# A streaming SwiGLU kernel: rows packed four to a slot, 64 KiB store descriptors, all transfers on one queue

## The chip, the cores and the metric

One core of a Trainium2 chip. Times are device microseconds (us) of whole executions; the profile's span is about 1.8 us shorter than the time of the same execution.

## The reference

```python
x = np.random.randn(8192, 8192).astype(np.float32)   # fixed seed
a, b = np.split(x, 2, axis=-1)
out = a * (b / (1 + np.exp(-b)))                      # 8192 x 4096 float32
```

268.4 MB are read, 134.2 MB are written, and each element is computed once.

## The kernel before

Two rows of x lie side by side in each of the 128 partitions (64 KiB), three such slots take turns. ACT computes silu in place, DVE multiplies in place, and the result is stored from the slot's front half. Loads are issued from the SP queue, nearly all stores from the ACT queue.

```python
R, BUFS = 2, 3
xv = x.tensor.reshape([N // R, R * M]).ap()
ov = out.tensor.reshape([N // R, R * half]).ap()
...
def load(i, rows=None):          # SP queue, 128 x 64 KiB
    ...
    nc.sync.dma_start(out=tiles[i][:, lo*M : hi*M], in_=xv[i*P : (i+1)*P, lo*M : hi*M])

def store(i, c0=0, cw=R * half): # ACT queue, 128 x 32 KiB
    (nc.scalar if i < last - 1 else nc.sync).dma_start(
        out=ov[i*P : (i+1)*P, c0 : c0+cw], in_=tiles[i][:, c0 : c0+cw])

for i in range(BUFS):
    load(i)
for i in range(last):
    for k in range(R):
        swiglu(i, k)             # ACT silu in place, DVE multiply in place
    ...
    store(i)
    nxt = i + BUFS
    if nxt < last:
        load(nxt)                # waits until store(i) has landed
    ...                          # the last tile is loaded and stored in pieces
```

Of the kernel before, what the change touches and what calls it, by code (L numbers as in the profile page):

```python
# [1 line left out]

# [4 lines left out]

_SILU = mybir.ActivationFunctionType.Silu


@with_exitstack
def kernel(
    ctx: ExitStack,
    tc: tile.TileContext,
    x: bass.AP,
    out: bass.AP,
):




    nc = tc.nc
    N, M = x.shape
    half = M // 2
    P = nc.NUM_PARTITIONS
    R = 2
    BUFS = 3

    xv = x.tensor.reshape([N // R, R * M]).ap()  # L30
    ov = out.tensor.reshape([N // R, R * half]).ap()
    ntiles = N // (P * R)
    last = ntiles - 1

    pool = ctx.enter_context(tc.tile_pool(name="sbuf", bufs=BUFS))
    ctx.enter_context(tc.manual_schedule())
    tiles = {}

    def load(i, rows=None):
        if i not in tiles:  # L40
            tiles[i] = pool.tile([P, R * M], x.dtype, name="xt")
        lo, hi = (0, R) if rows is None else rows
        nc.sync.dma_start(  # L43
            out=tiles[i][:, lo * M : hi * M], in_=xv[i * P : (i + 1) * P, lo * M : hi * M]
        )

    def swiglu(i, k, c0=0, cw=half):
        xt = tiles[i]
        b = xt[:, k * M + half + c0 : k * M + half + c0 + cw]
        nc.scalar.activation(out=b, in_=b, func=_SILU)  # L50
        nc.vector.tensor_mul(  # L51
            out=xt[:, k * half + c0 : k * half + c0 + cw],
            in0=xt[:, k * M + c0 : k * M + c0 + cw],
            in1=b,
        )

    def store(i, c0=0, cw=R * half):
        (nc.scalar if i < last - 1 else nc.sync).dma_start(
            out=ov[i * P : (i + 1) * P, c0 : c0 + cw], in_=tiles[i][:, c0 : c0 + cw]
        )  # L60

    for i in range(BUFS):
        load(i)
    for i in range(last):
        for k in range(R):
            swiglu(i, k)
        if i == last - 1:
            swiglu(last, 0)
        store(i)
        nxt = i + BUFS  # L70
        if nxt < last:
            load(nxt)
        elif nxt == last:
            load(last, (0, 1))
            load(last, (1, 2))

    store(last, 0, half)
    for c0 in range(0, half, half // 2):
        swiglu(last, 1, c0, half // 2)
    store(last, half, half)  # L80


# [1 line left out]
_INS = ['x']  # L84
_OUTS = [((8192, 4096), 'float32')]


# [23 lines left out]
```

## Time and profile before

| | before |
|---|---|
| time, median | 936.1 us |
| span of the profiled run | 934.8 us |
| busy: DVE, ACT | 30%, 25% |
| DMA engines, in 100 to 880 us | share 1.00, 434 to 435 GB/s |
| bytes moved | 402.67 MB |
| store on ACT queue, issue to landing | 39.7 us, one every 29 us |

Read it as a transfer-bound kernel: the 16 DMA engines never rest, and the computing fits beside them three times over. The lines behind the table stand in the prediction.

### The profile page before, as it was taken

Reading aid. Unit: us, or ns where it says so; the run is one execution under the profiler, and the core shown is the slowest. Engines: PE = TensorE matmul, PEld = TensorE weight load, DVE = VectorE, ACT = ScalarE, POOL = GpSimd, SP = SyncE. Lnnn points to the kernel's source line nnn. Section 1 sums busy time; section 2 is a strip of 40 time slices with the busy share of each in tenths; the row PEclk is TensorE's granted clock in tenths of the full one; section 3 lists DMA queues with packets and bytes.
Section 4 is the critical chain, followed back from the end, with each engine's and each line's share of the span. In section 5 each row is a group of like instructions: output and inputs, shape, how many; then the busy total and the mean of one; then the engine's idle time right before and its main releaser. Section 6 shows DMA issues by size and latency. Waiting matters only on the chain.

```text
span 934.8 us, 367 instructions
## 1 busy us (share of the span) xinstructions
DVE 283.3 (30%) x65; ACT 229.4 (25%) x66; POOL 0.2 (0%) x4
## 2 busy tenths in 40 slices
DVE  0333312333123331133321333213332133331242
ACT  0223320233302333113331133311333203332041
POOL 0000000000000000000000000000000000000000
DMA  9999999999999999999999999999999999999998
GB/s 404 400 445 430 430 439 433 428 435 443 428 430 439 429 442 432 435 426 453 419 430 452 411 452 423 428 447 425 433 433 453 414 443 429 426 447 428 425 437 376
DMA packets 9506, 402.67 MB, mean 431 GB/s; under 512 B 1056, under 2 KB 1056, under 8 KB 1056
## 3 DMA queue, kind: packets, MB, share of 16 engines
q1 hardware_dynamic: 5184, 276.83, 68.6%
q10 hardware_dynamic: 4320, 125.83, 31.2%
q14 instruction: 2, 0.02, 0.0%
HBM read 268.44 MB, written 134.22 MB: 431 GB/s over the span
## 4 chain that ended last, share of the span: by engine, by line
DMA 84%; DVE 10%; ACT 4%; DVEq 0%; issue 0%; SPq 0%; ACTq 0%
DMA out_dram<-xt 42%; DMA xt<-in_x_dram 42%; DVE xt L51 10%; ACT xt L50 4%; DVEq L106 0%; SPq L43 0%; ACTq L50 0%; DVEq L51 0%
## 5 line engine op out<-in xcount | busy, mean ns | idle before, releaser
L51 DVE TENSOR_TENSOR xt<-xt 128x4096 f32<-128x4096 f32 (+1 forms) x65 | 283.3, 4359 | 637.7 <-ACT xt L50 634.5
L50 ACT ACTIVATE xt<-xt 128x4096 f32<-128x4096 f32 (+1 forms) x65 | 228.1, 3556 | 688.1 <-DMA xt<-in_x_dram 688.1
L50 ACT ACT_TABLE_LOAD x1 | 1.3, 1283 | 0.7 <-PEq L95 0.7
L95 POOL MEMSET const-bfloat16-1.0<- 128x1 bf16 x1 | 0.1, 103 | 0.0
L95 POOL MEMSET const-uint8-127<- 128x1 uint8 x1 | 0.1, 102 | 0.0
L95 POOL MEMSET const-float32-0.0<- 128x1 f32 x1 | 0.1, 100 | 0.2 <-issue 0.2
L95 POOL MEMSET const-float32-1.0<- 128x1 f32 x1 | 0.1, 99 | 0.0
## 6 DMA issues: line engine op xcount, KB each, us to landing
out_dram<-xt ACTq DMA_DIRECT2D x30, 4096.0 KB, 39.7
xt<-in_x_dram SPq DMA_DIRECT2D x2, 4096.0 KB, 27.1
out_dram<-xt SPq DMA_DIRECT2D x1, 4096.0 KB, 23.6
out_dram<-xt SPq DMA_DIRECT2D x2, 2048.0 KB, 14.5
xt<-in_x_dram SPq DMA_DIRECT2D x31, 34.5
```

The lines of the kernel that those rows point to most:

```text
L50: nc.scalar.activation(out=b, in_=b, func=_SILU)
L51: nc.vector.tensor_mul(out=xt[:, k * half + c0 : k * half + c0 + cw], in0=xt[:, k * M + c0 : k * M + c0 + cw], in1=b,)
L95: nc = _bacc.Bacc("TRN2", target_bir_lowering=False, num_devices=1)
```

## The change

Intent: a store of four rows at once has 64 KiB per partition instead of 32 KiB, so there are half as many store descriptors. For this, four rows are loaded in two loads (the "pack" and the "extra"), and the results of the extra are written by DVE into the half of the pack that has become free. All transfers go to the SP queue in the order store, extra load, pack load.

```diff
-    R = 2
-    BUFS = 3
+    ngroups = N // (4 * P) - 1
...
+    extra = pool.tile([P, 2 * M], x.dtype, name="extra")
+    packs = [pool.tile([P, 2 * M], x.dtype, name=f"pack{s}") for s in range(2)]
...
+    load_pack(0)
+    load_extra(0)
+    load_pack(1)
+    for g in range(ngroups):
+        pack = packs[g % 2]
+        for k in range(2):
+            swiglu(pack, k, pack, k)
+        for k in range(2):
+            swiglu(extra, k, pack, 2 + k)
+        rows = o4[g * P : (g + 1) * P, :]
+        nc.sync.dma_start(out=rows, in_=pack)
+        load_extra(g + 1)
+        if g + 2 <= ngroups:
+            load_pack(g + 2)
...  (the last two tiles are loaded and stored in pieces, as before)
```

More of the change, by code (lines that the diff above doesn't have):

```diff
@@ L26 @@
     P = nc.NUM_PARTITIONS
-    R = 2
-    BUFS = 3
-    xv = x.tensor.reshape([N // R, R * M]).ap()
-    ov = out.tensor.reshape([N // R, R * half]).ap()
-    ntiles = N // (P * R)
-    last = ntiles - 1
-    pool = ctx.enter_context(tc.tile_pool(name="sbuf", bufs=BUFS))
-    ctx.enter_context(tc.manual_schedule())
-    tiles = {}
-    def load(i, rows=None):
-        if i not in tiles:
-            tiles[i] = pool.tile([P, R * M], x.dtype, name="xt")
-        lo, hi = (0, R) if rows is None else rows
-        nc.sync.dma_start(
-            out=tiles[i][:, lo * M : hi * M], in_=xv[i * P : (i + 1) * P, lo * M : hi * M]
-        )
@@ L47, in swiglu @@
-    def swiglu(i, k, c0=0, cw=half):
-        xt = tiles[i]
-        b = xt[:, k * M + half + c0 : k * M + half + c0 + cw]
+    ngroups = N // (4 * P) - 1
+    x4 = x.tensor.reshape([N // 4, 4 * M]).ap()
+    o4 = out.tensor.reshape([N // 4, 4 * half]).ap()
+    x2 = x.tensor.reshape([N // 2, 2 * M]).ap()
+    o2 = out.tensor.reshape([N // 2, 2 * half]).ap()
+    pool = ctx.enter_context(tc.tile_pool(name="sbuf", bufs=1))
+    ctx.enter_context(tc.manual_schedule())
+    extra = pool.tile([P, 2 * M], x.dtype, name="extra")
@@ L50, in swiglu @@
+    packs = [pool.tile([P, 2 * M], x.dtype, name=f"pack{s}") for s in range(2)]
+    def swiglu(src, k, dst, d, c0=0, cw=half):
+        b = src[:, k * M + half + c0 : k * M + half + c0 + cw]
         nc.scalar.activation(out=b, in_=b, func=_SILU)
         nc.vector.tensor_mul(
-            out=xt[:, k * half + c0 : k * half + c0 + cw],
-            in0=xt[:, k * M + c0 : k * M + c0 + cw],
+            out=dst[:, d * half + c0 : d * half + c0 + cw],
+            in0=src[:, k * M + c0 : k * M + c0 + cw],
@@ L54, in swiglu @@
             in1=b,
         )
-    def store(i, c0=0, cw=R * half):
-        (nc.scalar if i < last - 1 else nc.sync).dma_start(
-            out=ov[i * P : (i + 1) * P, c0 : c0 + cw], in_=tiles[i][:, c0 : c0 + cw]
-        )
-    for i in range(BUFS):
-        load(i)
-    for i in range(last):
-        for k in range(R):
-            swiglu(i, k)
-        if i == last - 1:
-            swiglu(last, 0)
-        store(i)
-        nxt = i + BUFS
-        if nxt < last:
-            load(nxt)
-        elif nxt == last:
-            load(last, (0, 1))
-            load(last, (1, 2))
@@ L77, with load_pack, load_extra @@
-    store(last, 0, half)
+    def load_pack(g):
+        if g < ngroups:
+            src = x4[g * P : (g + 1) * P, : 2 * M]
+        else:
+            src = x2[2 * ngroups * P : (2 * ngroups + 1) * P, :]
+        nc.sync.dma_start(out=packs[g % 2], in_=src)
+    def load_extra(g):
+        if g < ngroups:
+            nc.sync.dma_start(out=extra, in_=x4[g * P : (g + 1) * P, 2 * M :])
+        else:
+            r0 = (2 * ngroups + 1) * P
+            for k in range(2):
+                nc.sync.dma_start(
+                    out=extra[:, k * M : (k + 1) * M], in_=x2[r0 : r0 + P, k * M : (k + 1) * M]
+                )
@@ new lines @@
+    load_pack(0)
[5 more added lines that the diff above has]
+            swiglu(pack, k, pack, k)
+        for k in range(2):
+            swiglu(extra, k, pack, 2 + k)
[4 more added lines that the diff above has]
+            load_pack(g + 2)
+    pack = packs[ngroups % 2]
+    r0 = 2 * ngroups * P
+    for k in range(2):
+        swiglu(pack, k, pack, k)
@@ L78 @@
+    swiglu(extra, 0, extra, 0)
+    nc.sync.dma_start(out=o2[r0 : r0 + P, :], in_=pack[:, :M])
+    r0 += P
+    nc.sync.dma_start(out=o2[r0 : r0 + P, :half], in_=extra[:, :half])
     for c0 in range(0, half, half // 2):
-        swiglu(last, 1, c0, half // 2)
-    store(last, half, half)
+        swiglu(extra, 1, extra, 1, c0, half // 2)
+    nc.sync.dma_start(out=o2[r0 : r0 + P, half:], in_=extra[:, half:M])
 _INS = ['x']
```

## The prediction

> **What bounds the kernel now.** I read the slices of the page first, then the table by stage, then the timeline of one stage, then the waits.
>
> The slices and the DMA part of the page:
>
> ```profile
> DVE  0333312333123331133321333213332133331242
> ACT  0223320233302333113331133311333203332041
> DMA  9999999999999999999999999999999999999998
> DMA packets 9506, 402.67 MB, mean 431 GB/s; under 512 B 1056, under 2 KB 1056, under 8 KB 1056
> q1 hardware_dynamic: 5184, 276.83, 68.6%
> q10 hardware_dynamic: 4320, 125.83, 31.2%
> ```
>
> See that the 16 DMA engines are busy in all 40 slices, while DVE and ACT are idle for about 70%. The two queues' packets fill 68.6 + 31.2 = 99.8% of the engines' time: no second resource hides behind them.
>
> The table by stage (stretch and its length, busy time of DVE, ACT, POOL, clock, DMA share, GB/s):
>
> ```profile
> 0.00:1.00 1.00, 0.00 (x0) 0.28 (x1) 0.20 (x4) 1.00 0.00 0
> 23.40:46.70 23.30, 8.85 (x2) 6.59 (x3) 0.00 (x0) 1.00 0.99 401
> 100.00:500.00 400.00, 123.91 (x28) 99.72 (x28) 0.00 (x0) 1.00 1.00 435
> 500.00:880.00 380.00, 115.05 (x26) 92.59 (x26) 0.00 (x0) 1.00 1.00 434
> 932.00:934.80 2.80, 0.00 (x0) 0.00 (x0) 0.00 (x0) 1.00 0.07 29
> ```
>
> See that 780 of the 935 us run at a DMA share of 1.00 and 434 to 435 GB/s. Only the edges differ: no transfer in the first microsecond (the second has them), 401 GB/s in the stretch in which the first store meets the loads, and almost nothing in the last 2.8 us.
>
> The timeline of one stage gives the beat of the loop:
>
> ```profile
> 220.52 7.12 ACT L50 ACTIVATE xt<-xt 128x4096 f32<-128x4096 f32 x2 [21.89 <-DMA xt<-in_x_dram]
> 224.16 8.96 DVE L51 TENSOR_TENSOR xt<-xt 128x4096 f32<-128x4096 f32 x2 [20.06 <-ACT xt L50]
> 233.15 0.34 ACTq L58 DMA_DIRECT2D out_dram<-xt  x1
> 249.51 7.12 ACT L50 ACTIVATE xt<-xt 128x4096 f32<-128x4096 f32 x2 [21.87 <-DMA xt<-in_x_dram]
> ```
>
> See a new tile every 249.51 - 220.52 = 28.99 us. From a tile's landing to the issue of its store are 233.15 - 220.52 = 12.63 us, and after that ACT waits 21.9 us for the next load.
>
> The waits, of the compute engines and of the SP queue:
>
> ```profile
> ACT xt L50 <- DMA xt<-in_x_dram: 688.1, 33, 22.5
> SPq L43 <- DMA out_dram<-xt: 869.3, 29, 67.8
> ```
>
> See that SP nearly always waits for a store to land before it may reload that slot. This looks like a slot shortage, but the DMA share of 1.00 says that other queued transfers cover it. The chain of waits (42% store, 42% load) is that same queueing seen through the slots.
>
> The whole is 32 tiles x 28.99 = 927.7 us, and 7.1 us of edges. Of these about 2.0 lie before the first byte, about 1.8 in the slow stretch (23.3 x (1 - 401/434)), about 2.6 at the end (2.8 x 0.93), and some 0.7 are unassigned.
>
> **What the Trainium skill says.** First, "DMA: Bandwidth & Descriptors", section "Where 436 GB/s comes from": 16 ports x 32 B x 850 MHz make 435.2 GB/s. The trace agrees (434 to 435 in the steady stages). Bytes moved are 402.65 MB, so an estimate of the floor from that figure is 402.65 MB / 435.2 GB/s = 925.2 us. The kernel is 9.6 us of span, 1%, above a floor that includes no start, no end and no descriptor cost.
>
> Second, the same page, "Issuing engines are not separate DMA queues": issuing from several engines saves only the sequencer's issue time, as all run on the same 16 DMA engines. The trace agrees: in the steady stages a load descriptor takes the same 2418 ns whether or not the other queue has work, and the engines alternate without a gap. One issue costs 0.33 us, off the path.
>
> Third, the same page, "Latency and other measured facts", row "HBM row pitch at large powers of two": copies of 16 KiB rows at a pitch of 512 KiB between partitions ran at 207 GB/s a direction, against a full 214, and far lower at 2 MiB and more. The change loads rows of 64 KiB at a pitch of 128 KiB, where before the pitch was 64 KiB. No run here shows that pitch yet; it is below the smallest that the row found slow.
>
> **The change part by part.**
>
> *Bytes.* None removed: x is read once and out is written once. This caps everything at the 1% above.
>
> *Store descriptors.* The one thing truly removed. The packet records have three sizes, with medians of 2418 ns for 64 KiB, 1213 ns for 32 KiB, 611 ns for 16 KiB. Two halves cost 2 x 1213 = 2426, so joining two saves 8 ns on one engine. Per group of four rows (two tiles of before), an engine does 16 loads x 2418 + 16 stores x 1213 = 58.10 us before, and 16 x 2418 + 8 x 2418 = 58.03 us after; with one completion packet of 9 ns fewer the saving is 0.073 us, and over 15 groups 1.1 us. A second working, from the beat: two tiles take 57.98 us, 0.16 us above 25.17 MB / 435.2 GB/s = 57.83; spread over 32 descriptors and 4 completions that is 4.4 ns each, 9 of them fewer per group, 0.04 us, 0.6 us over 15 groups. I take 0.9 us.
>
> *Compute.* The order of instructions shows the same 65 activations of mean 3556 ns and 65 multiplications of mean 4359 ns; the last two of each four multiplications read the extra tile and write the pack. Change in time: none.
>
> *Slots and waits.* Still 192 KiB a partition (two packs, one extra), but other waits. Call the transfers of group g S (store), E (extra load), P (pack load). SP issues S(g), E(g+1), P(g+2). S(g) and E(g+1) both wait until the extra of g is computed; P(g+2) waits until S(g) has landed. All three are 8.39 MB, 8 descriptors an engine, 8 x 2418 = 19.34 us. Does the one queue ever run dry?
> - When E(g) lands, P(g+1) is next in the queue and covers 19.34 us. The store is issued 12.63 us later, and its first byte follows about 1.25 us after issue (first load issued at 0.73, first bytes at about 2.0). That is 13.9 us; slack 19.3 - 13.9 = 5.4 us, less a microsecond for the landing to be seen and up to 2 for engines ahead of others. About 3 us are left.
> - When S(g) lands, E(g+1) covers 19.34 us, and P(g+2) needs 0.33 + 1.25. Slack about 17 us.
> So every wait is covered and adds 0.
>
> *Moved: the store issue from ACT to SP.* ACT loses 30 issues of 0.34 us, about 10 us, but it idles 688 us. Worth 0. SP blocks in order, but S(g+1) cannot be ready before P(g+2) has been issued: S(g) lands about one transfer before E(g+1).
>
> *Edges.* The start is the same three loads of 8.39 MB. At the end, when the last half load lands, there are 4.19 + 2.10 + 2.10 MB of stores to run, as now, 19.3 us, and the last computing (about 8 us) fits beside the first 14.5. Change 0.
>
> Sum: 936.1 - 0.9 = **935.2 us**.
>
> **The rivals.**
>
> *A: turns between loads and stores cost time.* Before, load and store descriptors alternate on two queues, and stores are never absent once begun: each takes 39.7 us to land, and a new one comes every 29. The only turn from loads alone to stores, in 23.4 to 46.7, costs 1.5 to 1.8 us. After, each engine turns twice per group: 8 loads' or stores' worth of one kind, then the other. If each of 15 turns to stores cost 1.6 us, the time would be 935.2 + 14 x 1.6 = 958 us, slower by 2.3%. Against it: before, each engine switches between the kinds at nearly every descriptor at 435 GB/s, so a switch as such is free, and in the tail load and store descriptors follow each other on one queue without a gap. A little, 0.1 us a turn, would make 938.
>
> *B: the queue runs dry behind S.* The 3 us of slack could be smaller than thought, if landing is seen late. Missing 1 us per group would make 935 + 15 = 950; but compute durations are steady to some 20 ns, and I see nothing that takes 3 us. If only the engines that are ahead run dry, the end doesn't move.
>
> *C: the pitch of 128 KiB slows loads.* At the 3% that the skill's row has at 512 KiB, two thirds of the time would grow: 620 x 0.03 = 19 us, 954 us. For it: only the similar power of two. Against it: the pitch is four times smaller.
>
> *D: a little is gained at the edge.* The first store now queues behind a load rather than breaking in beside it; if that removes the 1.6 us, 933.6.
>
> **Range and chances.** Main path 80%: 933.5 to 936. Small costs of A to C 14%: up to 940. One of them in full 5%: about 950 to 958. Faster than 917.4 would need less than the floor of 925.2, so 1%, for a misread. Range 933 to 938.5; faster 0.01, same 0.94, slower 0.05.
>
> **What would show it.** Right: DMA nines throughout; about 57.9 us from one group to the next (activation of extra to the next); one queue only, at 99.7% of the engines, with the store descriptors at 2418 ns. Issue to landing about 26 us for the store (some 5 left of P, 19.3, 1), 45 for the extra, 39 for the pack. SP waits for DVE before the store and for the store before the pack load. The chain of waits is led by the extra load, with two multiplications (15%) and an activation (6%) per group. Wrong: a DMA share under 0.98 in the steady stages (B), descriptors over 2418 ns at each turn (A), or loads over 2418 ns throughout (C).

## The result, and the profile after

| | before | after |
|---|---|---|
| time, median of 6 runs | 936.29 us | 940.9 us |
| lowest to highest | 935.9 to 937.33 | 940.35 to 942.11 |
| span of the profiled run | 934.8 us | 938.6 us |

The ratio is 1.0049, interval 1.0037 to 1.0062. Ratios in this document are the mean time of one kernel's fast runs over that of the other's in the same rounds, so not quite the ratio of the medians quoted. The change is half a percent slower: inside 2%, but outside the predicted range of 933 to 938.5, and on the other side of the kernel before.

The slices and queues of the page, then the DMA issues (count, KB where given, median us from issue to landing):

```profile
DMA  9999999999999999999999999999999999999997
q1 hardware_dynamic: 7344, 402.66, 99.5%
...
pack<-in_x_dram SPq DMA_DIRECT2D x16, 38.8
extra<-in_x_dram SPq DMA_DIRECT2D x15, 45.2
out_dram<-pack SPq DMA_DIRECT2D x15, 26.4
```

One queue now fills the engines, and the three latencies are those foreseen (39, 45, 26). The waits (total, times, longest, us) and the chain's shares by engine:

```profile
ACT extra L44 <- DMA extra<-in_x_dram: 483.7, 17, 32.1
...
SPq L80 <- DVE pack L45: 471.3, 15, 31.7
SPq L57 <- DMA out_dram<-pack: 360.7, 14, 27.1
```

```profile
DMA 77%; DVE 14%; ACT 6%; SPq 1%; issue 0%; DVEq 0%; ACTq 0%
```

SP waits for the last multiplication before a store and for the store before a pack load, as in the working. The schedule does what it was designed to do, and yet the span grew by 3.8 us.

The chain of waits in order of time, with the lines that begin each group's extra (start us, us, what):

```profile
101.47 3.62 ACT extra L44
...
160.22 3.63 ACT extra L44
...
218.97 3.62 ACT extra L44
...
277.85 3.63 ACT extra L44
...
394.68 3.62 ACT extra L44
...
452.65 3.62 ACT extra L44
...
510.83 3.63 ACT extra L44
...
568.83 3.62 ACT extra L44
```

The early groups take 160.22 - 101.47 = 58.75 us, then 58.75 and 58.88; from 394.68 on 57.97, 58.18 and 58.00. Two tiles of before took 57.98. So the loop loses 0.8 us a group in the beginning, then almost nothing. A cost that fades is not the cost of a size or of an address.

The table by stage has the second loss, at the end (the line of before stands in the prediction: 2.8 us at 0.07):

```profile
100.00:500.00 400.00, 123.28 (x28) 99.72 (x28) 0.00 (x0) 1.00 1.00 433
...
932.00:938.60 6.60, 0.00 (x0) 0.00 (x0) 0.00 (x0) 1.00 0.26 109
```

For its last 6.6 us the kernel moves 109 GB/s: a few of the 16 engines still have descriptors to move while the others have finished.

The trace's packet records tell which. They can be strung together into 16 chains, one for each engine, since a packet starts within a few ns of the end of the one before (459 packets each after, 594 before, 25.17 MB, idle by some 0.3 us at most). A string can swap two engines, so the values for the worst engine are rough. "Lengthening" below is the sum, over an engine's packets, of what they took beyond the usual 2418, 1213 or 611 ns:

```
                                              before   after
lengthening, mean of the 16 engines, us         2.18    4.60
lengthening, the worst engine, us               3.2     8
last engine's end minus the mean end, us        1.26    3.34
first to last engine's end, us                  1.81    4.71
```

The mean grew by 2.4 us and the lag of the last engine by 2.1; 4.5 us, less the 0.6 to 1.1 that fewer descriptors were reckoned to save, gives the 3.8 measured. After the first 0.77 us at the start of the kernel, the lengthening sits almost wholly in one place: the last load descriptor ahead of each store, where an engine turns from loading to storing.

```
turn (group)             1     2     3     4     5     6     7     8
mean lengthening, us   1.07  0.44  0.19  0.29  0.36  0.20  0.10  0.05
engines apart by, us    0.5   1.0   1.3   2.0   3.4   3.6   3.6   3.4
```

("Apart" is the spread of the engines' starts on that descriptor.) At first all 16 engines turn within half a microsecond and all pay. Then they drift apart, and mainly those that come late go on paying: summed over the 16 turns, the eight earliest pay 2.6 us each and the four latest 5.3 us. The kernel before has one such place, its first store: about 1.5 us there, and 0.05 us in all afterwards.

### The profile page after: what moved, and what is told of

Same layout as the page of the kernel before. It is cut to its first block, busy times and chain, and to the rows that moved or that the text cites. A ratio compares the mean times of both kernels' runs of the same rounds, so it can differ in the third digit from the quotient of the medians.

```text
span 938.6 us, 324 instructions
## 1 busy us (share of the span) xinstructions
DVE 281.9 (30%) x65; ACT 229.4 (24%) x66; POOL 0.2 (0%) x4
## 4 chain that ended last, share of the span: by engine, by line
DMA 77%; DVE 14%; ACT 6%; SPq 1%; issue 0%; DVEq 0%; ACTq 0%
DMA extra<-in_x_dram 77%; DVE pack L45 14%; ACT extra L44 6%; SPq L80 1%; DVE extra L45 0%; DVEq L121 0%; SPq L66 0%; SPq L57 0%; ACTq L44 0%; SPq L62 0%
## 5 line engine op out<-in xcount | busy, mean ns | idle before, releaser
L45 DVE TENSOR_TENSOR pack<-extra 128x4096 f32<-128x4096 f32 x30 | 131.4, 4422 | 427.7 <-ACT extra L44 427.7
L44 ACT ACTIVATE extra<-extra 128x4096 f32<-128x4096 f32 (+1 forms) x33 | 114.2, 3505 | 483.7 <-DMA extra<-in_x_dram 483.7
L45 DVE TENSOR_TENSOR pack<-pack 128x4096 f32<-128x4096 f32 x32 | 141.6, 4425 | 191.0 <-ACT pack L44 189.3
L44 ACT ACTIVATE pack<-pack 128x4096 f32<-128x4096 f32 x32 | 114.0, 3608 | 208.2 <-DMA pack<-in_x_dram 208.2
L45 DVE TENSOR_TENSOR extra<-extra 128x2048 f32<-128x2048 f32 (+1 forms) x3 | 8.9, 3001 | 24.1 <-ACT extra L44 24.1
## 6 DMA issues: line engine op xcount, KB each, us to landing
pack<-in_x_dram SPq DMA_DIRECT2D x16, 38.8
extra<-in_x_dram SPq DMA_DIRECT2D x15, 45.2
out_dram<-pack SPq DMA_DIRECT2D x15, 26.4
```

Source lines behind the costliest of these rows:

```text
L44: nc.scalar.activation(out=b, in_=b, func=_SILU)
L45: nc.vector.tensor_mul(out=dst[:, d * half + c0 : d * half + c0 + cw], in0=src[:, k * M + c0 : k * M + c0 + cw], in1=b,)
```

## The experiments

Two rival theories stood at the start. **T1**: what costs is a store phase that begins on all engines together after a stretch of loads, whatever the queue. **T2**: what costs is a load followed by a store on one ring. And **T3**: the packing itself, by pitch or by descriptor size. The first four runs shared a chip and the runs of before (936.12 us).

### Stores on the ACT queue

```diff
-        nc.sync.dma_start(out=rows, in_=pack)
+        nc.scalar.dma_start(out=rows, in_=pack)
```

> The changed kernel with the 15 group stores issued from the ACT queue, nothing else changed. The packet records of the changed kernel show no idle engine, but the last load descriptor ahead of each store phase lengthened (1.07 us at the first turn, 0.45, 0.19, 0.29, 0.36 at the next ones, fading later), most on one or two engines that end 4 us late. T1, store phases that begin on all engines together after a stretch without stores slow the loads in flight, whatever the queue: the stores still pause some 19 us in each 58 us group, so the time stays at 939 to 942 and the lengthened load descriptors stay. T2, a load followed by a store on one ring is what costs: two rings interleave as in the kernel before, the lengthening goes except at the very first store, 934.5 to 936. T3, the 64 KiB store descriptors or the 128 KiB pitch cost: as the changed kernel, 940.5 to 941.5, with the lengthening spread over all descriptors of that kind.

Measured: 968.22 us, ratio 1.0346. Neither theory expected this: the lengthening does not stay or go but grows, to 24.6 us on average over the engines. SP's waits and the timeline show what came on top:

```profile
SPq L57 <- DMA out_dram<-pack: 616.5, 14, 50.2
```

```profile
156.98 0.33 SPq L57 DMA_DIRECT2D pack<-in_x_dram  x1
159.42 7.12 ACT L44 ACTIVATE extra<-extra 128x4096 f32<-128x4096 f32 x2 [27.04 <-DMA extra<-in_x_dram]
```

The store shares the engines with the extra load and lands late, so the next pack load is issued only 2.4 us before the extra load has been seen to land. The engines stood idle for 9.8 us on average in the whole run. So the run doesn't decide against T2: some engines ran dry, and that is what the lengthening goes with. After the first store (1.2 us) there are 14 more turns. Between the load ahead of the turn being issued and the turn itself, no engine was idle in two of them, and the turn cost 0.10 and 0.04 us on average over the engines; in the other 12 at least two engines were, and it cost 0.89 to 1.66. Another 6 us or so lie at the restarts themselves. The engines began these stores 0.7 to 3.1 us apart, so the cost did not need all of them to turn at one moment.

### The same schedule without the packing

```diff
-            src = x4[g * P : (g + 1) * P, : 2 * M]
+            src = x2[2 * g * P : (2 * g + 1) * P, :]
...  (the extra likewise from tile 2g+1)
-        nc.sync.dma_start(out=rows, in_=pack)
+        for h in range(2):
+            nc.sync.dma_start(out=o2[(2*g+h)*P : (2*g+h+1)*P, :], in_=pack[:, h*M : (h+1)*M])
```

> The changed kernel's schedule and single queue, but with the row mapping of the kernel before: each load is 128 x 64 KiB from one contiguous 8.39 MB block, and the group store is two stores of 128 x 32 KiB. No packing, no 64 KiB store descriptor, no 128 KiB pitch is left. T1 and T2 (the phase order or the single ring costs): 940 to 942, lengthened load descriptors ahead of the store phases remain. T3 (pitch or descriptor size): back to 935.5 to 937.

Measured: 939.79 us, ratio 1.0040. No 64 KiB store and no 128 KiB pitch is left, and nearly all of the cost remains (1.0049 and, in a later batch, 1.0036 for the changed kernel). T3 falls: the mapping isn't what costs. In the records the first turn costs 1.2 us, and the later ones don't simply fade: the sixth costs 0.56 and the tenth 0.32. Whether 30 stores of 32 KiB descriptors are slower than 15 of 64 KiB can't be told from the time at this noise.

### The kernel before on one queue

```diff
-        (nc.scalar if i < last - 1 else nc.sync).dma_start(
+        nc.sync.dma_start(
...
         store(i)
-        nxt = i + BUFS
+        nxt = i - 1 + BUFS
+        if i == 0:
+            continue
```

> The kernel before with all stores on the SP queue, each load issued one tile later so that SP does not block (order store i+1 after store i, then the load into slot i). Tiles, descriptors and addresses as before, but 31 turns from a load phase to a store phase, each of 9.7 us, in place of interleaving. T1 and T2: a cost at each of twice as many turns, 941 to 948. T3: 935.5 to 937, as none of the packing is in it.

Measured: 940.31 us, ratio 1.0043, a little below the expected 941 to 948. The old tiles, slots, addresses and descriptors, and the same loss as the whole change. The stage table of its end:

```profile
932.00:937.70 5.70, 0.00 (x0) 0.00 (x0) 0.00 (x0) 1.00 0.19 80
```

The same lagging engines: the last ends 3.3 us after the mean (1.3 in the kernel before). Twice the turns did not double the cost, as the first turn pays nearly half: 1.15 us there, then under 0.2 at each, and almost nothing in the second half of the run. The edit also moves each load to one tile later, so the queue and this order were changed together.

### Store and extra load alternated in halves

```diff
-        nc.sync.dma_start(out=rows, in_=pack)
-        load_extra(g + 1)
+        for h in range(2):
+            nc.sync.dma_start(out=rows[:, h*M : (h+1)*M], in_=pack[:, h*M : (h+1)*M])
+            nc.sync.dma_start(out=extra[:, h*M : (h+1)*M], in_=x4[..., (2+h)*M : (3+h)*M])
```

> The changed kernel on one queue, group store and extra load cut into halves of 4.19 MB and alternated: store half, extra half, store half, extra half, pack. Two turns from loads to stores per group in place of one. T2 (each load-to-store adjacency on the ring costs): twice the turns, 943 to 947. T1 (what matters is a stretch without stores before a burst): the long pause (29 us in place of 38.7) stays once per group, the second turn follows a pause of 9.7 us and costs less, 940 to 944. T3 by store descriptor size: 936 (all stores are 32 KiB here); by pitch: 941.

Measured: 939.37 us, ratio 1.0038; below what either theory expected. It doesn't tell them apart, beyond this: more turns are not more cost. The first is again 1.02 us, the later ones under 0.2. All group stores here have 32 KiB descriptors, and the loss is there.

### Engines brought back together once per group

The second batch (before: 936.71 us) tests what the fading suggested to me. **T1b**: all engines turning at one moment is what costs. **T1a**: the cost seen with stores on ACT was the waking of an idle queue. A one-column copy makes each pack load wait for the extra load too; the queue then runs dry once per group and all engines restart together.

```diff
         if g + 2 <= ngroups:
+            nc.gpsimd.tensor_copy(out=pack[:, 0:1], in_=extra[:, 0:1])
             load_pack(g + 2)
```

> The changed kernel, with a one-column copy on GpSimd from the extra tile into the pack that makes each pack load wait until the extra load has landed too. The queue runs dry for 2 to 3 us once per group, so all 16 engines start each pack load together and meet the store behind it together; still one queue. If the cost of a turn is that all engines begin storing at the same moment (T1b), the lengthening of the last load descriptor ahead of every store is again about 1 us on average over the engines, at all 15 turns, rather than 1.07 at the first and under 0.4 later; the time is about 940.9 + 14 x 2.5 + 14 x 0.8 = 985 us, and 975 without the lengthening. If it was the waking of an idle second queue that cost 1.7 us per group with the stores on ACT (T1a), the turns here stay under 0.4 us on average and the time is about 975.

Measured: 993.5 us (one run, its state unknown), correct. The timeline shows the first pack load and a later one, both issued into an empty queue:

```profile
0.74 0.38 SPq L57 DMA_DIRECT2D pack<-in_x_dram  x1
...
22.44 7.12 ACT L44 ACTIVATE pack<-pack 128x4096 f32<-128x4096 f32 x2 [20.42 <-DMA pack<-in_x_dram]
```

```profile
163.49 0.33 SPq L57 DMA_DIRECT2D pack<-in_x_dram  x1
...
186.66 7.12 ACT L44 ACTIVATE pack<-pack 128x4096 f32<-128x4096 f32 x2 [16.32 <-DMA pack<-in_x_dram]
```

From issue to computing the first takes 22.44 - 0.74 = 21.70 us, the later one 186.66 - 163.49 = 23.17. Only the second has a store waiting behind it. In the records each pack load of this run is longer in two places: at its first descriptor by 0.62 to 0.75 us, as at the start of the kernel, and at its last, ahead of the store, by 1.08 to 1.21 us on average, at all 14 turns that follow a restart, with the engines 0.5 to 0.8 us apart. The 1 us at every turn is what T1b expected. But the edit did two things at once: it brought the engines together, and it let the queue run dry 8 load descriptors ahead of each turn. This run can't tell the two apart, so a cost of waking a queue, near to T1a, isn't excluded. (The sum expected is 987, not 985. Against the changed kernel the span grew by 53.1 us; the records have 32.4 of idle engines, 9.7 of restarts, which I had not counted, 13.9 more at the turns, and a lag of the last engine that is 2.9 smaller: it ends only 0.4 us after the mean.)

### A store with no load in flight

```diff
-        for k in range(2):
-            swiglu(pack, k, pack, k)
+        if g == 0:
+            for k in range(2):
+                swiglu(pack, k, pack, k)
+        for k in range(2):
+            swiglu(packs[(g + 1) % 2], k, packs[(g + 1) % 2], k)
         for k in range(2):
             swiglu(extra, k, pack, 2 + k)
```

> The changed kernel with the computing of the next pack put ahead of that of the extra, so that each group store is issued only after the pack load has landed and been computed: the queue is empty when the store starts, no load is in flight. The time is far longer, some 300 us, and is not the point. If loads in flight are what a beginning store phase delays (T1), no load descriptor is lengthened by over 0.1 us at the turns, and the store descriptors take 2418 ns from the first. If starting to write is slow in itself, the first store descriptors of each group take 1 us longer.

Measured: 1291.99 us (one run, its state unknown). The first store descriptors are longer by only 0.05 to 0.07 us, so beginning to write is not slow in itself. Not foreseen: the last store descriptor, ahead of the extra load behind it, is longer by 0.72 to 0.80 us on average. Here the engines are within 0.16 us of each other (except at the last group), the turn is the other way round, from storing to loading, and again it is the first turn after the queue has run dry. In the run with restarts, where a turn from loads lies between the restart and this one, it cost under 0.04 us with the engines 0.6 us apart or more. So "loads in flight delayed by stores" was too narrow; whether closeness or the restart matters is not shown. The first load descriptors behind the turn are longer too, by up to 0.18 us.

### The packing, with stores in halves on the ACT queue

```diff
-        nc.sync.dma_start(out=packs[g % 2], in_=src)
+        for h in range(2):
+            nc.sync.dma_start(out=packs[g % 2][:, h*M : (h+1)*M], in_=src[:, h*M : (h+1)*M])
...
-        nc.sync.dma_start(out=rows, in_=pack)
+        for h in range(2):
+            nc.scalar.dma_start(out=rows[:, h*M : (h+1)*M], in_=pack[:, h*M : (h+1)*M])
```

> The changed kernel's packing and addresses, with the group store cut into two stores of 32 KiB descriptors issued from the ACT queue and the pack load cut into two halves, each waiting for its half of the store. Stores then alternate with loads one to one over the whole group and hardly pause. T1 (a cost only where stores begin anew beside loads): lengthened descriptors only at the first store, 935 to 937, as the kernel before. If the packing, the pitch or the slots cost in themselves: 939 or more.

Measured: 936.52 us, ratio to the kernel before 0.9999 (0.9987 to 1.0012). The packs, the extra slot and the pitch are those of the changed kernel, and the loss is gone. The end of its stage table:

```profile
932.00:934.70 2.70, 0.00 (x0) 0.00 (x0) 0.00 (x0) 1.00 0.06 24
```

No lagging engines (the last ends 1.0 us after the mean), and the records show lengthening at the start of the kernel (0.63 us) and at the first store (0.80), and under 0.04 at any other transfer.

But the run is not what it was built to be. Two store issues that follow each other:

```profile
113.18 0.36 ACTq L82 DMA_DIRECT2D out_dram<-pack  x1
...
158.88 0.34 ACTq L82 DMA_DIRECT2D out_dram<-pack  x1
```

No store of this run takes over 35.7 us to land, so at least 10 us between these two pass without any. In the packet records the stores pause for 16.7 to 19.0 us ahead of each of the 14 later groups. Then all 16 engines begin to store, within 0.4 us of each other in four groups and within 1.5 us in all of them, and pay 0.00 to 0.04 us on average. Long phases of loads and a common turn are both still there and cost nothing. That contradicts T1 and T1b, and it is the strongest single result. What differs from the changed kernel is the second queue, with loads running on beside the stores, and the halves. Half stores and half extra loads on one queue kept the loss (the contiguous and the alternating run), so the halves are not what helped, unless it was those of the pack loads.

### The changed kernel again

> The changed kernel unchanged, on the same chip as the runs beside it: 940 to 942. The lengthened load descriptors ahead of the stores should recur at the same places (largest at the first turn), and the engines that end last should differ from those of the first profile if the lag is chance, or be the same ones if it lies in the engines.

Measured: 939.55 us (938.89 to 941.45), ratio 1.0036; a little faster than on the first occasion, and the intervals overlap. The first turn costs 1.03 us again; the next ones 0.14, 0.14, 0.03 and 0.15, so how fast the cost fades differs from run to run. The last engine ends 3.7 us after the mean. Whether the same engines lag can't be said: the records don't name an engine, so that part of what I set out to see stays open.

### Engines kept apart at the first turn

```diff
+    nc.sync.dma_start(out=packs[1][0:8, :], in_=x4[0:8, : 2 * M])
     load_pack(0)
     load_extra(0)
     load_pack(1)
```

> The changed kernel with one more small load at the very front, 8 partitions x 64 KiB, into a place that is loaded over later. It gives 8 of the 16 engines one descriptor (2.4 us) more, so that the engines come to the first turn from loads to stores in two groups 2.4 us apart instead of all within 0.5 us. If the cost of a turn is that all engines turn at the same moment, the lengthening at the first turn falls from 1.03 to 1.07 us on average to about 0.5 or less, the later group paying more than the earlier. If each engine pays at its own turn whatever the others do, it stays at about 1.05. The time is expected at 940 to 943 either way, as 8 engines have 2.4 us more to do and those that are late pay at later turns.

Measured: 949.24 us, ratio 1.0139; slower than expected. At the first turn the lengthening is 0.00 us (1.03 to 1.07 without the stagger), and 0.11 and 0.04 us in the two groups after it. T1b expected 0.5 or less. But every engine's first descriptor took 5.1 to 6.4 us longer, and at three later turns 0.5 to 0.8 us came back, on all engines. The trace is that of the fastest of the four runs (945.13 us; the others took 949.16 to 950.00), so the records, with the slow start and 2.4 us of extra work on half the engines, explain that one and not the whole 13 us.

The obvious suspect for the slow start was that two loads read the same rows. The second version reads other rows:

```diff
-    nc.sync.dma_start(out=packs[1][0:8, :], in_=x4[0:8, : 2 * M])
+    nc.sync.dma_start(out=packs[1][0:8, :], in_=x4[1024:1032, 2 * M :])
```

> The staggered kernel again, its small front load now reading rows that no other load reads near that time. In the first staggered run every engine's first descriptor took some 5.5 us longer, which hid the rest: the front load and the first pack load read the same rows at once. If that was the reason, the start is back to about 0.7 us of lengthening here. The first turn should again show none (0 instead of 1.05 us in the changed kernel), as the engines turn in two groups one descriptor apart. Time 939 to 943: 8 engines have 2.4 us more to do, 1 us is saved at the first turn, and the later turns cost what the drift leaves. If the start stays at 5.5 us, the same rows were not the reason.

Measured: 949.08 us, ratio 1.0139. The stage table:

```profile
2.00:10.00 8.00, 0.00 (x0) 0.01 (x1) 0.00 (x0) 1.00 0.61 98
```

98 GB/s in the stretch of 2 to 10 us: the slow start is the same, so the shared rows were not its reason, and it stays unexplained. The first two turns again cost 0.00 us, the third 0.01. At the fourth and fifth 0.55 and 0.75 us came back, in both groups of engines, although they were still one descriptor apart as far as the records can be followed. Later 0.85 and 0.57 came back, and 0.88 at the last loads. After the start the engines lost 2.3 and 4.2 us on average in the two staggered runs, against 3.8 and 2.7 in the two profiles of the changed kernel: the cost was put off, not avoided.

## Why the prediction was wrong

**What held.** The bound, the bytes, the latencies of the three transfers (38.8, 45.2, 26.4 us against 39, 45, 26), the shares in the chain of waits (multiplications 14%, activations 6%), and the claim that no wait would leave the queue dry: the engines are idle by 0.07 us on average between their first and last packet. Rival B is out. So is rival C: the median load descriptor at the 128 KiB pitch took 2418 ns, as before, and the kernel without that pitch was no faster beyond noise. One sum is off by a hair without effect: two tiles lie 0.15 us, not 0.16, above 57.83. And "stores are never absent once begun" holds from issue to landing only.

**Store descriptors.** The 64 KiB store descriptor takes 2418 ns, as assumed. The 0.6 to 1.1 us saved are a computed amount; no run isolates them, but the records fit: the mean end of the engines moved by 1.68 us where the lengthening grew by 2.42, which leaves 0.74 saved.

**The step that failed.** It is the argument against rival A: "before, each engine switches between the kinds at nearly every descriptor at 435 GB/s, so a switch as such is free". So the prediction put the turns at 0. The reading was taken from a kernel with loads and stores on two queues, and carried over to turns within one queue. The records of the seven profiles whose engines are idle by under 0.1 us between their first and last packets, in us on average over the engines:

```
                               queues  first turn  all later turns  last engine's end minus the mean
kernel before                     2       1.5           0.05              1.3
packing, two queues               2       0.8           0.1               1.0
changed kernel                    1       1.1           2.4               3.3
changed kernel, again             1       1.0           1.3               3.7
without the packing               1       1.2           2.3               2.5
kernel before, on one queue       1       1.1           1.3               3.3
alternated halves                 1       1.0           1.2               2.5
```

On two queues the reading holds: once the first store is through, turns are free, even where all engines turn within 0.4 us after 17 us or more of loads. On one queue it fails in every kernel: 3.4 us at the turns of the changed kernel against 1.5 before. Shown at this level in both directions: the old kernel put on one queue loses 4 us (940.31), the new one put on two, in halves, loses nothing (936.52). My first account, that all engines turning at one moment is what costs, does not survive the record: in the packing on two queues they turn together for nothing, and with stores on ACT they paid 0.89 to 1.66 us while up to 3.1 us apart.

**Its size.** Rival A in full, 1.6 us at each of 15 turns, would have been 958 us. The mean over the engines was 3.4 us for all 16 turns, 0.21 a turn, the first of them 1.07. The prediction did have a small version, "0.1 us a turn, would make 938" (that needs both turns of a group; 14 turns alone make 936.6), and 14% for small costs up to 940; its range stopped at 938.5. It also named the sign, descriptors over 2418 ns at the turns, and that is what came.

**"Edges. Change 0."** Wrong too, and about half of the loss. The late engines pay more than the others, turn after turn; in a queue that never ran dry they did not catch up, while in the run that ran dry in every group the last one ended 0.4 us after the mean. The time is that of the last one. Its lag behind the mean went from 1.26 to 3.34 us, and the table by stage shows it as 6.6 us at a DMA share of 0.26.

**Rival D**, a gain at the first store, came in part: 1.49 us before became 1.07 in the changed kernel, and 0.80 in the packing on two queues. The later turns took more than that back.

**What stays open.** Why turns cost on one queue: because a store follows a load on one ring (T2), or because no load runs on beside the stores. No run separates these two; one queue with loads and stores in turn at every descriptor would, or two queues with stores alone in a phase and no idle engine. What a restart does: about 1 us was paid at the first turn after the start of the kernel in nine profiles (0.80 to 1.49), and at turns after a restart in two runs (0.89 to 1.66), but the staggered runs paid nothing at their first one, and no run changed the restarts alone. Why late engines pay more, and what slowed the start of the staggered runs. That the lag follows from the turns is argued from the order of payment; no run removed the lag alone. No version beat the kernel before: the packing on two queues equals it.

## What to carry to other kernels

A cost that is read as zero where loads and stores have a queue each need not be zero where they share one: here one queue cost 0.4 to 0.5% in each of four kernels. A second queue is no gain by itself, though: with the order of waits that lets engines run dry it cost 3.5%. And check in the trace that an experiment made the condition it was built for; the one whose stores were to "hardly pause" had pauses of 17 us and more, and its trace overturned the account it was meant to support. A DMA share of 1.00 doesn't rule out loss in the transfers themselves: compare the time from one group to the next, early and late in the run, with bytes over rate. Look at the last microseconds too, since 16 engines that never idle can still finish far apart, and the slowest one sets the time.

## What the Trainium skill lacked or had wrong

- "DMA: Bandwidth & Descriptors", "Issuing engines are not separate DMA queues", says that several issuing engines save only sequencer time. The issue time itself was indeed off the path, but here the choice of queue, with the order that goes with it, moved the time: the kernel before went from 936.12 to 940.31 us on one queue, the packing took 939.55 on one and 936.52 on two, and the changed kernel with its stores alone moved to a second queue ran at 968.22.
- I found on no page what a turn from loads to stores costs: 0.80 to 1.49 us on average over the engines at the first turn of nine profiles, 1.08 to 1.21 at all 14 turns of the run in which the queue ran dry ahead of each, 1.2 to 2.4 at all later turns together on one queue, and at most 0.1 on two queues that never ran dry.
- "DMA: Bandwidth & Descriptors", "Latency and other measured facts", begins its row on HBM row pitch at 512 KiB. Here a 128 KiB pitch of 64 KiB rows cost nothing: 2418 ns a descriptor, as at 64 KiB.
- The pages give latencies of a single DMA, but I found on none how much longer the first descriptor of a queue that has run dry takes: 0.62 to 0.75 us for loads and 0.05 to 0.08 for stores, and behind a small load on 8 partitions at the start of the kernel 5.1 to 6.4 us.
